# Weights of the values projection loaded into idle stage tiles, their splits between halves of a block, and gates stepped at each row tile

## The chip, the cores and the metric

The kernel runs on one core of a Trainium2 chip. The time is the device time of one execution in microseconds (us); lower is better. A run of the kernel gives one time, and the median over several runs is shown. Engines are named as in the profile: PE is TensorE (PEld its weight loads), DVE is VectorE, ACT is ScalarE, POOL is GpSimd. SP (SyncE) issues most of the DMAs; the rest are issued from ACT's and POOL's queues.

## The reference, cut to what matters

One encoder layer on x of 2048 rows by 1024 columns, in float32. The change lies in the first sub-layer's input projection and beside it:

```
hn = rms_norm(x, norm_mix_pre)
proj = hn @ w_in                          # 2048 x 3600
cv = short_conv3(proj[..., :2560], conv_w, conv_b)
q, k = silu(cv[..., 0:512]), silu(cv[..., 512:1024]) * 128 ** -0.5   # 4 heads
v, o_gate = proj[..., 2560:3072], sigmoid(proj[..., 3072:3584])
gates = proj[..., 3584:3600] + b_gates    # input and forget gates, two directions, 4 heads
h_m = (mlstm(q, k, v, gates[0], log_sigmoid(gates[1])) + mlstm backwards) * o_gate
z = cv[..., 1024:1536]                    # Hyena group
z = cv[..., 1536:2048] * two_sided_fft_conv(z, filter 0)
z = cv[..., 2048:2560] * two_sided_fft_conv(z, filter 1)
x = x + rms_norm(concat(group_rms(h_m), group_rms(z)) @ w_out, norm_mix_post)
x = x + rms_norm(square(relu(rms_norm(x) @ w_mlp_in)) @ w_mlp_out)
```

In the mLSTM, running sums of log_sigmoid of the forget gate and running maxima over chunks of 128 rows (16 chunks) are turned into weights and a stabiliser before any head can be worked on.

## The kernel before, in words

Nearly every large product is made as three matmuls: each operand is split into a high part, rounded to fp32r (a cast on ACT, line 166), and the remainder (a subtract on DVE or POOL, line 169), and `mm3` (lines 154 to 161) issues low x high, high x low and high x high.

**The projection** (`project`, line 328) is a Python generator in two parts. The convolved part (`convolved`, line 559) makes the first 2560 columns, transposed, in 20 column tiles of 128 by 4 blocks of 512 rows; a block is three pieces of 9, 9 and 6 matmuls. The values part (`values_project`, line 660) makes the last 1040 columns, rows by columns, in four groups g of 260 columns in the order 3, 0, 1, 2 by 16 row tiles t of 128 rows; a block (one g, one t) is two halves of 12 matmuls of 260 columns, for k tiles 0 to 3 and 4 to 7. The running number of a block, 0 to 63, is i. Groups 0 and 1 hold the values, the end of 1, 2 and 3 the output gate (a sigmoid on ACT), and the last 16 columns of group 3 the gates.

**The weights** (`in_weights`, line 530) come in chunks of up to 520 columns in total. `fetch` loads a chunk from SP's queue into one of two raw tiles (tag wf). `chunk` multiplies it by the norm's weight on POOL (line 543), then casts it on ACT and subtracts on DVE into a pair of tiles (tags w0 and w1, four buffers each). A group of the values part has four chunks q of two k tiles each, a column tile of the convolved part two. A fetch into a raw tile must wait until the earlier chunk's split has read it, and a cast until the matmuls of the chunk four earlier have read its tile.

At a change of group in the values part (lines 734 to 743), chunks 0 and 1 of the next group are fetched after row tiles 9 and 11. After row tile 15 both are scaled and split, and behind each split a fetch of chunk 2 or 3 is issued; then chunks 2 and 3 are scaled and split. The first steps of the generator, up to line 684, do the same for group 3 while the convolved part ends: its last calls of `next(then)` (lines 569, 630, 640, 651 and 658) step the values generator.

**What sets the order.** From line 294 on the order of instructions on each engine is the order of the code. `drive` (line 217) weaves two generators: the Hyena pass with the loads of the first mLSTM head (`long_conv`, line 334) leads, and for each unit of time that it yields, the projection is stepped until it has yielded as much. So a yield such as the 4.0 in line 741 is a claim of time: the Hyena pass gets that much before the next block. The Hyena pass loads its operands from SP's queue three steps ahead (tag raw, six buffers), splits them on ACT, POOL and DVE, multiplies spectra in five DVE instructions of 64 or 128 rows by 512 (`product`, line 1111), and stores from ACT's queue. When it ends, `head_loads` puts 1 MB each of k, v and q in SP's queue, and `turned` makes the weighted keys from k and the gates.

**Stage tiles.** A convolved block's output stands in one of four tiles of tag yc (512 columns) until it is stored. In the values part the first of them is `gtile`: half of it takes the gate columns (`gin`, written by line 713), the other half two constants. The gates (`gates`, line 753) use three more, cut in tiles of 128 columns. A values block's output goes to a tile of tag vst (two buffers, two row tiles each) and is stored to DRAM from SP's queue.

**The gates** are a generator too, of some 20 steps: small matmuls with constants, a chain of some 12 DVE instructions with two scans, exponentials on ACT, and three round trips through DRAM (st_d, m_d, de_d; a store from ACT's queue, a load from SP's) that move values from partitions to rows. `values_project` steps them at every second row tile from i = 18 on (line 744). The results are `qt` and `decay` and a row of maxima in DRAM, `mrow`.

Of the kernel before, what the change touches and what calls it, by code (L numbers as in the profile page):

```python
# [8 lines left out]
F32 = mybir.dt.float32  # L9
# [138 lines left out]
class Builder:  # L148
# [381 lines left out]
    def in_weights(self, c0, n):  # L530

        wv = self.io["w_in"].rearrange("(k p) c -> p k c", p=128)
        nk = min(8, 520 // n)

        def fetch(q):
            raw = self.pw.tile([128, 520], F32, tag="wf", name="wf")[:, 0:nk * n].rearrange("p (k c) -> p k c", k=nk)
            self.load(raw, wv[:, nk * q:nk * q + nk, c0:c0 + n])
            return raw, self.nw[:, nk * q:nk * q + nk]

        def chunk(fetched):  # L540

            raw, nw = fetched
            self.pool.tensor_tensor(raw, raw, nw.unsqueeze(2).to_broadcast([128, nk, n]), ALU.mult)
            w = [self.pw.tile([128, 520], F32R, tag=f"w{e}", name=f"w{e}", bufs=4)[:, 0:nk * n]
                 .rearrange("p (k c) -> p k c", k=nk) for e in range(2)]
            self.split(w[0], w[1], raw)
            return w

        return fetch, chunk, 8 // nk

    @staticmethod
    def row_block(chunks, k):
# [6 lines left out]
    def convolved(self, cts, then):  # L559

        wk, hn, cw = self.pw, self.hn, self.cw
        pe, dve, act, pool = self.pe, self.dve, self.act, self.pool
        n = 4 * len(cts)
        fetched, weights, pts, ys, sts = {}, {}, {}, {}, {}

        def ahead(c, step):

            if c >= len(cts):
                next(then)
                return  # L570
            fetch, chunk, m = self.in_weights(128 * cts[c], 128)
# [14 lines left out]

        def centre(i):
            ct, b = of(i)
            yc = ys[i] = wk.tile([128, 512], F32, tag="yc", name="yc", bufs=4)
            act.activation(yc, pts[i], AF.Identity, scale=cw[:, ct, 1:2], bias=cw[:, ct, 3:4])  # L590

        def sides(i):
# [14 lines left out]
        def gated(i):  # L607
            if of(i)[0] < 8:
                act.activation(ys[i], ys[i], AF.Silu)
# [24 lines left out]
        for i in range(n + 3):  # L634
# [20 lines left out]
                stored(i - 3)  # L655
            if 2 <= i <= n + 1:
                gated(i - 2)
            yield 1.36 if i < n - 1 else 1.36 * live + next(then)

    def values_project(self):  # L660
# [1 line left out]
        wk, act, dve, N = self.pw, self.act, self.dve, 260  # L662
        raws, chunks, pts, sts = {}, {}, {}, {}

        def fetch(g, q):
            raws[g, q] = self.in_weights(2560 + N * g, N)[0](q)

        def chunk(g, q):
            chunks[g, q] = self.in_weights(2560 + N * g, N)[1](raws.pop((g, q)))

        bg = self.cp_bg
        self.load(bg, self.io["b_gates"].partition_broadcast(128))
# [1 line left out]
        fetch(3, 0)  # L674
        fetch(3, 1)
        yield 0.0
        for q in range(2):
            chunk(3, q)
            fetch(3, q + 2)
            yield 0.0  # L680
        chunk(3, 2)
        yield 0.0
        chunk(3, 3)
        yield 2.0

        self.gtile = wk.tile([128, 512], F32, tag="yc", name="gtile", bufs=4)
        self.gin = self.gtile[:, 0:256].rearrange("p (k c) -> p k c", k=2)
        gates = self.gates()

        def width(g):  # L690
# [2 lines left out]
        def block(g, t, ks):  # L693
            if ks[0] == 0:
                pts[g, t] = self.pp.tile([128, 512], F32, tag="pp", name="pt")[:, 0:N]
            for k in ks:
                self.mm3(pts[g, t], self.hn_tile(t, k), self.row_block([chunks[g, q] for q in range(4)], k), k == 0, k == 7)
# [23 lines left out]
                          sts.pop((g, t // 2))[:, :, 0:n])  # L721

        before, last, steps = None, None, [(g, t) for g in order for t in range(16)]
        for i, (g, t) in enumerate(steps):
            block(g, t, range(0, 4))
            if last:
                outputs(*last)
            yield 1.4
            block(g, t, range(4, 8))
            if before:  # L730
                stored(*before)
            before, last = last, (g, t)
            yield 1.4
            nxt = steps[min(i + 7, len(steps) - 1)][0]
            if nxt != g and t in (9, 11):
                fetch(nxt, t // 11)
            if nxt != g and t == 15:
                for q in range(2):
                    chunk(nxt, q)
                    fetch(nxt, q + 2)  # L740
                yield 4.0
                for q in range(2, 4):
                    chunk(nxt, q)
            if i >= 18 and i % 2 == 0:
                next(gates, None)
        outputs(*last)
        stored(*before)
# [5 lines left out]
    def gates(self):  # L753
# [18 lines left out]
        for kind, gs in enumerate((li, lf)):  # L772
            pt = bank()[:, 0, :]
# [1145 lines left out]
```

## Time and profile before

| what | value |
| --- | --- |
| time before, median of 3 runs (lowest to highest) | 2744.96 us (2743.41 to 2745.59) |
| the profiled execution's own time | 2740.85 us |
| its span in the profile | 2738.9 us, 35521 instructions |
| convolved part, last matmul | 718.5 us into the span |
| values part, first to last matmul | 730.5 to 1043.4 us |
| scaling of a chunk of weights on POOL (line 543), 56 of them | median 1042 ns |
| mean granted clock of PE over the span | 0.981 |

How to read it: the profile records one execution, instruction by instruction. Times in the views are from the start of the span. A row such as "PE pt L159 <- ACT w L166: 9.6, 3, 5.3" says that PE's instruction of line 159 that writes tile pt waited for ACT's instruction of line 166 that writes tile w, 9.6 us in all, three times, the longest 5.3. In rows in order of time the bracket holds how long the engine had been idle, and what ended that. The granted clock is the share of its full rate at which PE could run; 1.00 is full. Names of tiles: hn the normalised input, w the split weights, pt a block's bank of PSUM, py, p, pk, pu and pi those of the Hyena pass.

### The profile page before, as it was taken

The page shows a single profiled execution, that of the slowest core. Times are in us where ns is not written, and L with a number is a line of the kernel's source. Part 1 is how long each engine was busy: PE and PEld are TensorE (multiplying, and loading weights), DVE is VectorE, ACT ScalarE, POOL GpSimd, SP SyncE. Part 2 cuts the span into 40 slices and gives each one's busy share as a digit, 9 for nine tenths or more (in the row PEclk, how much of TensorE's full clock was granted, in tenths as well). Part 3 has the DMA queues.
Part 4 walks back from the last instruction along what each step waited for, and adds up shares of the span by engine and source line. Part 5 has one row for each costly group of instructions (what it writes and reads, how often), then busy time and mean ns, then how long its engine had stood idle before and what let it go on. Part 6 is the DMA issues. An engine that isn't in the chain of part 4 may idle for free.

```text
span 2738.9 us, 35521 instructions
## 1 busy us (share of the span) xinstructions
PE 2604.2 (95%) x12293; PEld 2125.6 (78%) x12293; DVE 1529.3 (56%) x2453; ACT 1239.9 (45%) x2301; POOL 1218.2 (44%) x973
## 2 busy tenths in 40 slices
PE   6999999999899998889997999989999999999998
PEld 5778888777788887767775788868888888888876
DVE  5676653777446654765555444464445443543578
ACT  6355544555434445653433544354454233232244
POOL 1221124554225542456675877777773340311232
PEclk9999999999999999999998999989999999999999
DMA  6233346565665648546756444453446553445546
GB/s 173 59 97 107 113 122 226 183 191 175 203 216 180 191 156 273 166 145 209 239 165 220 149 168 143 167 210 139 162 144 253 176 182 110 123 143 164 181 160 222
DMA packets 288355, 465.76 MB, mean 170 GB/s; under 512 B 37542, under 2 KB 149414, under 8 KB 287152
## 3 DMA queue, kind: packets, MB, share of 16 engines
q1 hardware_dynamic: 227600, 324.85, 37.9%
q10 hardware_dynamic: 53264, 117.53, 11.4%
q0 software_dynamic: 7312, 21.11, 3.0%
q8 instruction: 98, 1.61, 0.2%
q14 instruction: 81, 0.66, 0.1%
HBM read 289.27 MB, written 174.13 MB: 169 GB/s over the span
## 4 chain that ended last, share of the span: by engine, by line
PE 40%; DVE 5%; POOL 3%; ACT 2%; DMA 2%; issue 2%; ACTq 0%; DVEq 0%; POOLq 0%; SPq 0%
PE pm L160 13%; PE pm L161 13%; PE pm L159 13%; DVE cb L169 1%; DVE hm L169 1%; POOL xt L1222 1%; ACT xo L1360 1%; DMA m<-in_w_mlp_out_dram 0%; DVE hm L1844 0%; POOL cb L169 0%; DVE xo L1363 0%; DMA hm<-ht 0%; ACTq L234 0%; DVE gss L1264 0%; POOL ht L1395 0%
## 5 line engine op out<-in xcount | busy, mean ns | idle before, releaser
L166 ACT CAST cb<-m 128x1024 fp32r<-128x1024 f32 (+1 forms) x346 | 281.3, 847 | 443.7 <-PE pm L159 388.6
L169 DVE TENSOR_TENSOR cb<-m,cb 128x1024 fp32r<-128x1024 f32 (+1 forms) x222 | 239.5, 1116 | 301.1 <-ACT cb L166 300.8
L160 PE MATMUL pm<-hm,cb 128*128 128x512 f32 x896 | 355.2, 396 | 18.8 <-DVE hm L169 14.7
L159 PE MATMUL pm<-hm,cb 128*128 128x512 f32 x896 | 354.5, 396 | 9.2 <-POOL cb L169 4.1
L161 PE MATMUL pm<-hm,cb 128*128 128x512 f32 x896 | 353.8, 395 | 0.0
L160 PE MATMUL pm<-cb 128*128 128x512 f32 x880 | 344.0, 391 | 6.5 <-DVE cb L169 6.5
L159 PE MATMUL pm<-cb 128*128 128x512 f32 x880 | 342.6, 390 | 1.0 <-DVE cb L169 1.0
L161 PE MATMUL pm<-cb 128*128 128x512 f32 x880 | 343.1, 390 | 0.0
L169 POOL TENSOR_TENSOR cb<-m,cb 128x1024 fp32r<-128x1024 f32 x124 | 268.7, 2180 | 71.0 <-ACT cb L166 71.0
L1656 DVE TENSOR_TENSOR m<-pm,m 128x512 f32<-128x512 f32 x224 | 154.4, 690 | 258.0 <-PE pm L161 231.3
L159 PE MATMUL pt<-hn,w 128*128 128x512 f32 x640 | 269.4, 421 | 1.0 <-ACT hn L486 0.9
L160 PE MATMUL pt<-hn,w 128*128 128x512 f32 x640 | 253.9, 397 | 0.7 <-DVE hn L487 0.7
L161 PE MATMUL pt<-hn,w 128*128 128x512 f32 x640 | 252.8, 395 | 0.0
L169 POOL TENSOR_TENSOR raw<-raw,hi 128x512 fp32r<-128x512 f32 x160 | 205.6, 1298 | 104.4 <-ACT hi L166 79.3
L160 PEld LDWEIGHTS pm<-hm,cb 128*128 128x128 f32 x896 | 170.6, 190 | 60.0 <-DVE hm L169 18.0
L159 PEld LDWEIGHTS pm<-hm,cb 128*128 128x128 f32 x896 | 170.7, 191 | 49.8 <-POOL cb L169 6.1
L160 PEld LDWEIGHTS pm<-cb 128*128 128x128 f32 x880 | 165.5, 188 | 44.0 <-DVE cb L169 9.8
L161 PEld LDWEIGHTS pm<-hm,cb 128*128 128x128 f32 x896 | 170.7, 191 | 36.3
L159 PEld LDWEIGHTS pm<-cb 128*128 128x128 f32 x880 | 165.4, 188 | 35.9 <-ACT junk L1829 1.4
L161 PEld LDWEIGHTS pm<-cb 128*128 128x128 f32 x880 | 165.6, 188 | 34.3
L1660 ACT ACTIVATE m<-m 128x512 f32<-128x512 f32 x128 | 80.5, 630 | 221.4 <-DVE m L1656 214.9
L159 PE MATMUL pt<-w,hn 128*128 128x260 f32 x512 | 156.8, 306 | 9.6 <-ACT w L166 9.6
(322 smaller groups left out, 5572.5 us busy)
## 6 DMA issues: line engine op xcount, KB each, us to landing
ga<-m ACTq DMA_DIRECT2D x96, 512.0 KB
m<-ga SPq DMA_DIRECT2D x96, 512.0 KB
d<-st ACTq DMA_DIRECT2D x64, 512.0 KB
m<-in_w_mlp_in_dram SPq DMA_DIRECT2D x62, 512.0 KB
m<-in_w_mlp_out_dram SPq DMA_DIRECT2D x114, 256.0 KB
raw<-d SPq DMA_DIRECT2D x96, 256.0 KB
xt<-in_x_dram SPq DMA_DIRECT2D x32, 512.0 KB
dk<-kst SPq DMA_DIRECT2D x32, 512.0 KB
```

The lines of the kernel that those rows point to most:

```text
L159: pe.matmul(ps, w[1], x[0], start=first, stop=False)
L160: pe.matmul(ps, w[0], x[1], start=False, stop=False)
L161: pe.matmul(ps, w[0], x[0], start=False, stop=last)
L166: self.act.copy(hi, src)
L169: (eng_lo or self.dve).tensor_tensor(lo, src, hi.bitcast(F32), ALU.subtract)
L1222: eng.tensor_tensor(res[:, cs], tmp[e], res[:, cs], ALU.add)
L1360: act.activation(x1, xt, AF.Square, accum_out=ss1[:, h:h + 1])
L1656: dve.tensor_tensor(dst, a, b, ALU.add)
L1660: act.activation(g, g, AF.Relu)
```

## The change

Five edits, all in the projection and the gates:

- `in_weights` gives the scaling as a function of its own, and `fetch` can be told another tile than the raw ones. Stage tiles become 520 columns wide so that a chunk fits.
- At a change of group, chunks 2 and 3 of the next group are fetched at row tiles 9 and 11 as well, into two stage tiles. For group 1 only chunk 2 is; its chunk 3 takes a raw tile after chunk 0's split. Chunks are scaled at row tiles 12, 13 and 14, and after 15.
- The casts and subtracts of chunks 0 and 1 stand between the two halves of the block of row tile 15, those of 2 and 3 behind it. The yield of 4.0 there is kept for group 1 alone, and one of 1.0 is added for all.
- The generator of the values is stepped once more, at the end of the convolved block n - 4, and its first steps are cut differently: a fetch of chunk 2 goes with chunk 1's split, one of chunk 3 a step later.
- The gates are stepped at every row tile from i = 18, and finished at i = 40 if they are not. `gtile` goes: the gate columns go to `qt`, whose final contents are written later, and `mt` becomes the tile of `cm`.

```diff
@@ in_weights
-        def fetch(q):
-            raw = self.pw.tile([128, 520], F32, tag="wf", name="wf")[:, 0:nk * n].rearrange("p (k c) -> p k c", k=nk)
+        def fetch(q, place=("wf", 2)):
+            raw = self.pw.tile([128, 520], F32, tag=place[0], name="wf", bufs=place[1])[:, 0:nk * n].rearrange("p (k c) -> p k c", k=nk)
...
-        def chunk(fetched):
+        def scale(fetched):
             raw, nw = fetched
             self.pool.tensor_tensor(raw, raw, nw.unsqueeze(2).to_broadcast([128, nk, n]), ALU.mult)
+
+        def chunk(fetched, scaled=False):
+            raw = fetched[0]
+            if not scaled:
+                scale(fetched)
             w = [self.pw.tile([128, 520], F32R, tag=f"w{e}", name=f"w{e}", bufs=4)[:, 0:nk * n]
...
@@ convolved
-            yc = ys[i] = wk.tile([128, 512], F32, tag="yc", name="yc", bufs=4)
+            yc = ys[i] = wk.tile([128, 520], F32, tag="yc", name="yc", bufs=4)[:, 0:512]
...
+            if i == n - 4:
+                next(then)
             yield 1.36 if i < n - 1 else 1.36 * live + next(then)
@@ values_project
         fetch(3, 0)
         fetch(3, 1)
         yield 0.0
-        for q in range(2):
-            chunk(3, q)
-            fetch(3, q + 2)
-            yield 0.0
+        chunk(3, 0)
+        yield 0.0
+        chunk(3, 1)
+        fetch(3, 2)
+        yield 0.0
+        fetch(3, 3)
+        yield 0.0
         chunk(3, 2)
         yield 0.0
         chunk(3, 3)
         yield 2.0
-        self.gtile = wk.tile([128, 512], F32, tag="yc", name="gtile", bufs=4)
-        self.gin = self.gtile[:, 0:256].rearrange("p (k c) -> p k c", k=2)
+        self.gin = self.qt[:, 0:2, :]
...
+        yc = "yc", 4
         for i, (g, t) in enumerate(steps):
+            nxt = steps[min(i + 7, len(steps) - 1)][0]
+            new = nxt != g
             block(g, t, range(0, 4))
             if last:
                 outputs(*last)
             yield 1.4
+            if new and t == 15:
+                chunk(nxt, 0, True)
+                chunk(nxt, 1, True)
             block(g, t, range(4, 8))
             if before:
                 stored(*before)
             before, last = last, (g, t)
             yield 1.4
-            nxt = steps[min(i + 7, len(steps) - 1)][0]
-            if nxt != g and t in (9, 11):
-                fetch(nxt, t // 11)
-            if nxt != g and t == 15:
-                for q in range(2):
-                    chunk(nxt, q)
-                    fetch(nxt, q + 2)
-                yield 4.0
-                for q in range(2, 4):
-                    chunk(nxt, q)
-            if i >= 18 and i % 2 == 0:
+            if i == 40:
+                for _ in gates:
+                    pass
+            if new and t == 9:
+                fetch(nxt, 0)
+                fetch(nxt, 2, yc)
+            if new and t == 11:
+                fetch(nxt, 1)
+                if nxt != 1:
+                    fetch(nxt, 3, yc)
+            if new and t in (12, 13, 14):
+                scale(nxt, t - 12)
+            if new and t == 15:
+                if nxt == 1:
+                    fetch(nxt, 3)
+                else:
+                    scale(nxt, 3)
+                chunk(nxt, 2, True)
+                if nxt == 1:
+                    yield 4.0
+                chunk(nxt, 3, nxt != 1)
+                yield 1.0
+            if i >= 18:
                 next(gates, None)
@@ gates
-        free = [self.gtile[:, 256:384], self.gtile[:, 384:512]]
+        free = []
         for _ in range(3):
-            t = self.pw.tile([128, 512], F32, tag="yc", name="gt", bufs=4)
+            t = self.pw.tile([128, 520], F32, tag="yc", name="gt", bufs=4)
...
-        rev, permt, li, lf, e, u, l1, rc, ones, bc, r, cm, mt = free[0:13]
+        rev, permt, li, lf, e, u, l1, rc, ones, bc, r, cm = free
+        mt = cm
...
-        dve.tensor_copy(mt, pt)
-        self.store(self.mrow, mt)
+        dve.tensor_copy(rc, pt)
+        self.store(self.mrow, rc)
```

More of the change, by code (lines that the diff above doesn't have):

```diff
@@ L547, in chunk @@
             return w
-        return fetch, chunk, 8 // nk
+        return fetch, chunk, 8 // nk, scale
     @staticmethod
@@ L570, in ahead @@
                 return
-            fetch, chunk, m = self.in_weights(128 * cts[c], 128)
+            fetch, chunk, m, _ = self.in_weights(128 * cts[c], 128)
             if step == 0:
@@ L663, in values_project, with fetch, scale, chunk @@
         raws, chunks, pts, sts = {}, {}, {}, {}
[L665 to L669, printed above, removed]
+        def fetch(g, q, *place):
+            raws[g, q] = self.in_weights(2560 + N * g, N)[0](q, *place)
+        def scale(g, q):
+            self.in_weights(2560 + N * g, N)[3](raws[g, q])
+        def chunk(g, q, scaled=False):
+            chunks[g, q] = self.in_weights(2560 + N * g, N)[1](raws.pop((g, q)), scaled)
         bg = self.cp_bg
```

## The prediction

> **What bounds the kernel now.** I read three views in turn: the page (which engine is full), the table by stretches over the projection's last 400 us (where that engine is not full), and the waits and rows in order of time there (what it waits for).
>
> ```profile
> PE 2604.2 (95%) x12293; PEld 2125.6 (78%) x12293; DVE 1529.3 (56%) x2453; ACT 1239.9 (45%) x2301; POOL 1218.2 (44%) x973
> ```
>
> The page says that PE is busy 95% of the span. In such a kernel a change that moves no matmul can win only stretches in which PE stands still, or runs at a lower clock. So the next view is where those are. Columns: window, length, busy time of PE, PEld, DVE, ACT, POOL, granted clock, DMA share, GB/s.
>
> ```profile
> 680.00:700.00 20.00, 20.00 (x85) 15.53 (x84) 8.67 (x16) 6.87 (x11) 0.00 (x0) 1.00 0.66 211
> 700.00:720.00 20.00, 18.35 (x76) 13.73 (x74) 12.08 (x19) 8.19 (x16) 8.18 (x7) 1.00 0.25 72
> 720.00:740.00 20.00, 13.89 (x70) 11.43 (x71) 10.52 (x19) 10.95 (x19) 5.88 (x5) 0.83 0.79 284
> 800.00:820.00 20.00, 14.52 (x107) 13.50 (x105) 5.35 (x13) 5.17 (x10) 2.06 (x2) 0.93 0.44 152
> 840.00:860.00 20.00, 20.00 (x139) 17.62 (x137) 14.61 (x29) 9.66 (x17) 7.75 (x8) 1.00 0.59 182
> 880.00:900.00 20.00, 17.59 (x104) 14.18 (x103) 14.60 (x25) 10.70 (x21) 13.38 (x14) 1.00 0.72 219
> 960.00:980.00 20.00, 14.67 (x82) 11.66 (x82) 13.31 (x21) 8.01 (x18) 12.11 (x12) 0.94 0.50 162
> 1040.00:1060.00 20.00, 13.55 (x87) 12.42 (x86) 4.75 (x10) 10.26 (x33) 2.52 (x5) 0.82 0.95 293
> ```
>
> PE is full in the rows from 680 and from 840. The holes are the hand-over from the convolved part to the values part (7.8 us idle in 700 to 740), the three changes of group in the values part (5.5, 2.4 and 5.3 us) and the start of the mLSTM (6.5 us). The waits say whose they are: total, times, longest.
>
> ```profile
> PE pt L159 <- ACT w L166: 9.6, 3, 5.3
> PE py L159 <- ACT hi L166: 5.5, 3, 3.5
> PE pk L159 <- ACT z L1104: 2.2, 1, 2.2
> PE pt L160 <- DVE w L169: 1.5, 3, 0.7
> SPq L231 <- DVE w L169: 24.4, 4, 11.1
> ```
>
> The first and fourth are PE waiting for the split of the next group's weights, the last is SP's queue standing still because a fetch of weights waits until a split has emptied its buffer. The rows in order of time put them in place (start, length, what, idle before it):
>
> ```profile
> 717.99 0.38 SPq L231 DMA_DIRECT2D wf<-in_w_in_dram  x1
> 723.10 0.50 PE L159 MATMUL py<-hi,c 128*128 128x512 f32 x1 [3.45 <-ACT hi L166]
> 812.68 1.03 SPq L231 DMA_DIRECT2D wf<-in_w_in_dram  x2
> 817.43 2.06 POOL L543 TENSOR_TENSOR wf<-wf,nw 128x520 f32<-128x520 f32 x2 [20.99 <-DMA wf<-in_w_in_dram]
> 819.19 0.58 PE L159 MATMUL pt<-w,hn 128*128 128x260 f32 x1 [5.25 <-ACT w L166]
> 896.27 0.39 PE L159 MATMUL pt<-w,hn 128*128 128x260 f32 x1 [1.73 <-ACT w L166]
> 971.47 0.47 PE L159 MATMUL pk<-hi,c 128*128 128x512 f32 x1 [2.22 <-ACT z L1104]
> 977.34 0.44 PE L159 MATMUL pt<-w,hn 128*128 128x260 f32 x1 [2.64 <-ACT w L166]
> ```
>
> At the first change of group the second half of the weights is fetched at 812.68, once the first half is split; it is scaled at 817.43, and PE starts at 819.19. That whole chain is what the change loads ahead. The hand-over's hole has another owner: a fetch of weights leaves SP at 717.99, behind a split, and the Hyena loads queued behind it come late to the cast on which PE waits until 723.10.
>
> Idle time is followed by matmuls at a lower clock (the third column from the end):
>
> ```profile
> 704.00:708.00 4.00, 2.98 (x13) 1.88 (x11) 1.94 (x4) 2.47 (x5) 2.12 (x2) 1.00 0.13 16
> 708.00:712.00 4.00, 3.73 (x15) 2.76 (x16) 1.83 (x3) 1.37 (x3) 0.00 (x0) 1.00 0.88 310
> 724.00:728.00 4.00, 1.62 (x3) 0.58 (x3) 1.90 (x3) 2.56 (x5) 2.42 (x3) 0.62 0.87 321
> 728.00:732.00 4.00, 3.77 (x13) 3.28 (x14) 3.81 (x9) 2.64 (x6) 1.17 (x1) 0.53 0.45 151
> 819.20:822.00 2.80, 2.47 (x9) 2.17 (x10) 1.70 (x4) 2.48 (x7) 1.60 (x3) 0.50 0.24 84
> 822.00:826.00 4.00, 4.00 (x28) 4.00 (x28) 0.43 (x1) 0.89 (x2) 4.00 (x5) 0.76 0.59 171
> 976.00:980.00 4.00, 2.19 (x9) 1.94 (x10) 1.90 (x3) 1.86 (x5) 1.64 (x2) 0.69 0.61 211
> 980.00:984.00 4.00, 4.00 (x26) 3.75 (x26) 2.08 (x4) 2.64 (x7) 3.00 (x3) 0.88 0.32 94
> ```
>
> Busy time times what the clock lacks is the loss. It is 1.62 x 0.38 + 3.77 x 0.47 = 2.4 us at the hand-over, 2.47 x 0.5 + 4.00 x 0.24 = 2.2 us after the first change of group, and 2.19 x 0.31 + 4.00 x 0.12 = 1.2 us after the third.
>
> **The change part by part.** The costs of one chunk, and PE's pace (shortest, median, longest; below, two neighbouring matmuls of the values part):
>
> ```profile
> L543 POOL TENSOR_TENSOR wf<-wf,nw x56: 1033/1042/1498, 18.5 to 976.6; 128x512 f32<-128x512 f32 x40, 128x520 f32<-128x520 f32 x16
> L166 ACT CAST w<-wf x56: 607/621/640, 19.5 to 977.7; 128x512 fp32r<-128x512 f32 x40, 128x520 fp32r<-128x520 f32 x16
> L169 DVE TENSOR_TENSOR w<-wf,w x56: 675/692/1442, 22.7 to 978.3; 128x512 fp32r<-128x512 f32 x40, 128x520 fp32r<-128x520 f32 x16
> 1043.24 0.29 PE L160 MATMUL pt<-w,hn 128*128 128x260 f32 x1
> 1043.36 0.28 PE L161 MATMUL pt<-w,hn 128*128 128x260 f32 x1
> ```
>
> A matmul starts every 0.12 us, so half a block (12 of them) is 1.44 us. No arithmetic of the reference goes or comes: the same scalings, splits, fetches and matmuls are issued elsewhere.
>
> *Hand-over.* The values generator is stepped once earlier, so chunk 0 of group 3 is scaled and split one block earlier, while POOL is idle (0.00 in the row from 680), and the fetch of chunk 2 stands a step later than chunk 0's split, chunk 3's a step later than chunk 1's. Then neither waits in SP's queue, and the Hyena loads behind them leave when their buffers come free. The 3.45 us and most of the two stalls behind it go. What is late next: chunks 2 and 3 are still scaled and split among the Hyena operands, and the cast of chunk 2 waits on ACT for POOL. One chunk's passage (1.04 + 0.62 + 0.69 = 2.35 us) lies ahead of the next Hyena operand, so I keep that as a stall; I also keep the 1.3 us of small stalls between 704 and 712 (1.02 and 0.27 in the rows above), which are of the Hyena pass itself. Saved: 7.8 - 1.3 - 2.35 = 4.1 us idle and the 2.4 us of clock: 6.5 us. Bounds: 2 (SP's stall shrinks but operands stay late) to 10 (all).
>
> *First change of group* (3 to 0). All four chunks are in SBUF by row tile 11, two of them in stage tiles that nothing else uses then. The scalings lie on POOL, which has 2.1 us of work in 20 here. After the first half of block 15 the casts of chunks 0 and 1 start; DVE ends at about 0.62 + 2 x 0.69 = 2.0 us, while PE has 1.44 us of the second half and 0.72 us of chunk 0's k tiles. Chunks 2 and 3 follow in 2 x 0.69 more, by 3.5 us, and PE needs them at 2.9 and 3.6. The Hyena pass issues nothing here, since its next loads wait for stores. Saved: 5.5 idle and 2.2 of clock, 7.7 us; bounds 5 to 8.
>
> *Second change* (0 to 1). The gate tiles hold three of the four stage tiles, so only chunk 2 goes ahead; chunk 3 is fetched when chunk 0 is split, and its scaling queues on POOL behind two Hyena prepares, its subtract on DVE behind two Hyena products. That is the order of before, and I take the 2.4 us to stay; bounds -2 (one more product in front) to +2.4.
>
> *Third change* (1 to 2). Loaded ahead like the first; the gates are through by row tile 37, so the stage tiles are free at 41. In before the chunks' casts stand on ACT ahead of the copy of a spectrum, and wait there for POOL: that is the 2.22 us at 971.47, then 2.64 us for the second pair. In the new order POOL has scaled three of the four, and between block 15's first half and the first use of chunk 2 PE has two more Hyena products and three halves, about 6 us, against 3.5 us of splits. Saved: 5.3 idle and 1.2 of clock, 6.5 us; bounds 3 to 6.5.
>
> *Gates at each row tile.* 20 steps from row tile 18 now end at 37 and no longer at 56. The instructions are the same; store and load of each DRAM round trip stand two row tiles apart, and load and use one; 16 row tiles lie between the restarts at 819.19 and 896.27, so these are 9.6 and 4.8 us. I cost it at nothing: DVE has 14.61 us of work in 20 in the row from 840, and covers it; without that cover it is the slower rival below. Renaming two gate tiles (the running maximum in place, gin in the tile of the results) moves no instruction.
>
> *Order against the Hyena pass.* The generator now claims 1 + 5 + 1 units at the changes of group, where it claimed 4 + 4 + 4. So 5 units less of its time are empty, and values work runs ahead: counting the yields of both versions, 6 halves of blocks follow the loads of the first mLSTM head in before, 3 in after. The rows there:
>
> ```profile
> 1031.13 1.02 PE L1144 MATMUL pi<-z,ci 128*128 128x512 f32 x2
> 1032.80 0.33 ACTq L234 DMA_DIRECT2D d<-st  x1
> 1035.62 0.33 SPq L231 DMA_DIRECT2D k<-qk  x1
> 1047.71 2.45 PE L957 MATMUL pS<-q,k 128*128 128x128 f32 x16 [3.63 <-DMA q<-qk]
> 1048.66 0.67 ACT L708 ACTIVATE vst<-pt 128x260 f32<-128x260 f32 x2 [10.35 <-DMA vo<-vst]
> ```
>
> The last Hyena matmuls, their store, the loads of k, v and q and the first scores are one chain, 16.6 us from 1031.13 to 1047.71, and PE already waits 3.63 us for its end. Three halves now stand in front of that chain, not beside it: 3 x 1.44 = 4.3 us are given back, as more idle time before the scores. Against it, ACT's 10.35 us wait ends: the store that it waited for now goes ahead of the 3 MB of loads, so the head's casts and the last store come earlier. PE still waits for q, so I take only 1 us for it; bounds -1 to 5.
>
> **Sum.** 6.5 + 7.7 + 0 + 6.5 - 4.3 + 1 = 17.4 us. The profiled execution took 2740.85 us, 4.1 less than the median shown, and holes of this kind are in each execution; so the 17.4 goes off the median, 2744.96: about 2727.6 us.
>
> The Trainium skill, TensorE: Matmul & The Clock Gate (Part 1, What's actually happening), lets the clock fall only after an idle window of about 3.4 us. By that rule the third change, whose stalls are 2.22 and 2.64 us with matmuls between them, would have no clock to win back, and the sum would be 16.2 us, 2728.8. The rows from 976 (0.69 and 0.88) speak against a strict reading.
>
> **The rivals.** *Splits held on the in-order engines.* The early casts stand on ACT ahead of Hyena casts and wait there for PE to leave the weight tile. If that, or a product in front of them on DVE, costs at each change what the second costs now (2.4 us), the first and third win 5.3 and 4.1; with 4 at the hand-over, and nothing at the mLSTM's start, 4 + 5.3 + 4.1 - 4.3 = 9.1 us: 2735.9. For it: the row at 971.47 is such a case. Against it: at the first change the Hyena pass is silent, and at the third PE has 6 us of cover. The Trainium skill, TensorE: Matmul & The Clock Gate (Part 1, Architectural detail), states that ACT and DVE are strict FIFO, which is this rival's rule; the trace agrees at 971.47.
>
> *Given back.* Only the first change works (7.7), the hand-over stays bound by the Hyena operands, the third keeps its stalls because POOL comes late, and the end takes its 4.3: 3.4 us, 2741.6, no change by the measure below.
>
> *Slower: the gates on DVE.* Place: row tiles 18 to 37, 20 x 4.8 = 96 us, in which DVE has (20 - 14.61) / 20 of the time to spare, 26 us. A gate step has work of its own and makes DVE wait in order for a matmul, an exponential or a landing. Above 1.3 us in each of the 20 steps the spare time is gone, and Hyena products come late to PE. It eats the whole gain from 17.4 + 26 = 43 us on, 2.2 us a step; at 2.6 us a step (52 us) the loss is 26 us, net 8.6: 2753.6. Against it: before runs such a step at every second row tile there already, and PE is full in the row from 840.
>
> **How the numbers follow.** The forecast 0.64, splits held 0.22, given back 0.09, slower 0.05. About 0.2% (5.5 us) is what a measurement of this kernel can tell from no change. The forecast's own bounds, when not all of them fall together, are 2718 to 2734; the range goes up to take in the held splits: 2717 to 2740. Faster by over 0.2% (under 2739.5): 0.64 + 0.22 and a little of the third, 0.87; within 0.2%: 0.08; slower: 0.05.
>
> **What would show it.** In the profile after: SP's waits for DVE w gone; no PE wait for ACT w over 1 us at the first and third change, one of 1 to 3 us at the second; clock 1.00 after both; the first scores still waiting for q, for some 7 us or more; ACT's wait for the values store gone. The forecast is wrong if new PE waits for DVE or ACT appear between 820 and 930, where the gates now run, or if the mLSTM's start moves by less than 10 us.

## The result, and the profile after

| | before | after |
| --- | --- | --- |
| median (lowest to highest, runs) | 2745.47 us (2743.41 to 2747.03, 6) | 2719.70 us (2713.61 to 2724.55, 6) |
| profiled execution, its span | 2740.85 us, 2738.9 us | 2723.08 us, 2721.3 us |

The ratio is 0.9905, 95% interval 0.9894 to 0.9917: 25.8 us faster, where 17.4 were forecast. The two profiled executions differ by only 17.8 us, because the one of before lies 4.6 below its median and the one of after 3.4 above. That must be kept in mind when one trace is read against the other.

The engines in the page of after have the same work and a shorter span:

```profile
PE 2602.7 (96%) x12293; PEld 2125.3 (78%) x12293; DVE 1527.1 (56%) x2453; ACT 1237.2 (45%) x2300; POOL 1220.3 (45%) x973
```

The table by stretches of after, with the columns of the prediction's:

```profile
700.00:720.00 20.00, 17.95 (x69) 13.60 (x68) 11.62 (x20) 10.34 (x19) 8.37 (x8) 0.91 0.49 157
720.00:740.00 20.00, 19.78 (x114) 16.46 (x113) 11.81 (x21) 13.62 (x21) 6.34 (x6) 1.00 0.76 254
800.00:820.00 20.00, 20.00 (x160) 19.60 (x159) 5.74 (x15) 7.81 (x16) 5.96 (x6) 1.00 0.49 156
840.00:860.00 20.00, 20.00 (x133) 17.38 (x132) 14.59 (x28) 8.77 (x17) 11.85 (x12) 1.00 0.82 245
860.00:880.00 20.00, 19.54 (x123) 16.42 (x122) 13.58 (x26) 11.03 (x25) 11.31 (x11) 1.00 0.85 185
880.00:900.00 20.00, 17.51 (x106) 14.99 (x106) 14.15 (x29) 8.49 (x17) 10.18 (x11) 0.91 0.52 168
960.00:980.00 20.00, 20.00 (x137) 17.79 (x137) 14.29 (x22) 9.42 (x22) 11.71 (x11) 1.00 0.64 196
```

PE is now full in the rows from 800 (14.52 busy before) and from 960 (14.67 before), both at a clock of 1.00: the first and the third change of group have no hole left. The hand-over has 2.05 + 0.22 = 2.3 us idle where it had 7.8. What remains is in the row from 880, at the second change. DVE, which the slower rival feared for, is as busy in 840 to 860 as it was (14.59 against 14.61), and PE is full in that row.

The waits of after's SP queue from 690 to 1045, and of PE from 690 to 1095 (those that bear on the change, and the longest):

```profile
SPq L231 <- DVE w L169: 6.1, 1, 6.1
```

```profile
PE ps L1008 <- ACT nm L1015: 4.0, 3, 2.5
PE pt L159 <- ACT w L166: 2.1, 1, 2.1
PE ptk L945 <- DVE kw L952: 2.1, 1, 2.1
PE ptk L945 <- DMA k<-qk: 1.5, 1, 1.5
PE py L159 <- ACT hi L166: 1.0, 1, 1.0
PE pt L160 <- DVE w L169: 0.3, 1, 0.3
```

PE's first row lies inside the mLSTM. SP stood 24.4 us in four waits for a split to empty a buffer; it now stands 6.1 in one, where the prediction had none left. PE's three waits for the cast of the next weights have become one, at the second change. ACT's 10.35 us wait for a values store is gone. And there is a line that the prediction did not have: at the mLSTM's start PE waits 1.5 us for k and no longer for q. The rows in order of time (start, length, what, idle before it), all of after but the last, which is of before:

```profile
708.96 0.50 PE L159 MATMUL py<-hi,c 128*128 128x512 f32 x1 [1.03 <-ACT hi L166]
885.14 0.39 PE L159 MATMUL pt<-w,hn 128*128 128x260 f32 x1 [2.15 <-ACT w L166]
1027.87 0.63 PE L945 MATMUL ptk<-eye,k 128*128 128x128 f32 x4 [1.46 <-DMA k<-qk]
1030.57 1.12 PE L945 MATMUL ptk<-eye,k 128*128 128x128 f32 x4 [2.06 <-DVE kw L952]
1036.52 1.06 PE L990 MATMUL pS<-q,k 128*128 128x128 f32 x8
1043.48 0.60 PE L912 MATMUL ptk<-eye,k 128*128 128x128 f32 x4
```

The keys of the first head are transposed on PE (ptk) and then scaled. After turns twelve of the sixteen ahead of the first scores (pS), which then wait for nothing. In before only the four of the row at 1043.48 went ahead, and the scores waited 3.63 us for q.

**Two points that divide the time.** The last Hyena product (pi) and the last product of the mLSTM (pa) are the same matmuls in both kernels. Their groups, before and then after; the two numbers behind the durations are the starts of the first and the last one:

```profile
L1144 PE MATMUL pi<-z,ci x128: 590/592/592, 495.7 to 1031.6; 128*128 128x512 f32 x128
L977 PE MATMUL pa<-v,pm x256: 272/275/422, 1068.9 to 1191.7; 128*128 128x129 f32 x128
```

```profile
L1177 PE MATMUL pi<-z,ci x128: 590/592/668, 497.2 to 1018.6; 128*128 128x512 f32 x128
L1010 PE MATMUL pa<-v,pm x256: 272/275/422, 1047.5 to 1173.8; 128*128 128x129 f32 x128
```

Hyena, first to last: 535.9 us before, 521.4 after. From there to the first pa: 37.3 before, 28.9 after; to the last pa: 160.1 before, 155.2 after. Everything behind it is alike: pa ends 17.9 us earlier, the span 17.6.

The second stretch in one row for each kernel, from the last pi to the end of the mLSTM, before and then after:

```profile
1031.60:1192.40 160.80, 134.28 (x921) 121.14 (x919) 97.26 (x263) 97.08 (x328) 65.34 (x75) 0.95 0.62 198
```

```profile
1018.60:1174.40 155.80, 132.63 (x884) 119.81 (x882) 96.34 (x263) 96.21 (x326) 65.20 (x75) 0.92 0.65 203
```

The counts show the halves of blocks: 921 matmuls against 884 are the three halves of 12 that now run earlier (one record is missing). So 4.3 us of work have left this stretch, as forecast. But PE's idle time in it did not rise by them: it is 26.5 us before and 23.2 after. The clock is lower in this one execution of after (0.92), which hides a part of the gain.

### The profile page after: what moved, and what is told of

Same layout as the page of the kernel before. It is cut to its first block, busy times and chain, and to the rows that moved or that the text cites. A ratio compares the mean times of both kernels' runs of the same rounds, so it can differ in the third digit from the quotient of the medians.

```text
span 2721.3 us, 35529 instructions
## 1 busy us (share of the span) xinstructions
PE 2602.7 (96%) x12293; PEld 2125.3 (78%) x12293; DVE 1527.1 (56%) x2453; ACT 1237.2 (45%) x2300; POOL 1220.3 (45%) x973
## 4 chain that ended last, share of the span: by engine, by line
PE 40%; DVE 5%; POOL 3%; DMA 3%; ACT 2%; issue 2%; ACTq 0%; DVEq 0%; POOLq 0%; SPq 0%
PE pm L160 13%; PE pm L161 13%; PE pm L159 13%; DVE cb L169 1%; POOL xt L1255 1%; DVE hm L169 1%; ACT xo L1393 1%; DMA m<-ga 1%; DVE hm L1877 0%; DMA m<-in_w_mlp_out_dram 0%; POOL cb L169 0%; DMA hm<-ht 0%; DVE xo L1396 0%; POOL ht L1428 0%; DVE hm L1807 0%
## 5 line engine op out<-in xcount | busy, mean ns | idle before, releaser
L169 DVE TENSOR_TENSOR cb<-m,cb 128x1024 fp32r<-128x1024 f32 (+1 forms) x222 | 232.5, 1084 | 306.0 <-ACT cb L166 296.3
L635 POOL DMA_DIRECT2D vp<-vst x96 | 61.3, 642 | 232.0 <-ACT vst L631 230.9
```

The source lines that it names most:

```text
L169: (eng_lo or self.dve).tensor_tensor(lo, src, hi.bitcast(F32), ALU.subtract)
L635: pool.dma_start(dst[:, 8 * b + e:8 * b + 8:2, cc:cc + 128], st[64 * e:64 * e + 64])
```

## The experiments

Theory A is the recorded sum: the holes give 20.7 us, three halves of blocks are given back at the mLSTM's start (4.3), and 1 is won there. Theory B: the start of the mLSTM itself became shorter, so the price of 4.3 is none; it first named ACT's wait for the values store as the cause. The kernel before was run again beside each group of experiments, with medians of 2748.76, 2751.69 and 2750.38 us on three chips; so ratios are compared, and 0.0010 is 2.7 us.

**The hand-over alone**, in the kernel before, and **the change without it**:

```diff
+            if i == n - 4:
+                next(then)
...
-        for q in range(2):
-            chunk(3, q)
-            fetch(3, q + 2)
-            yield 0.0
+        chunk(3, 0)
+        yield 0.0
+        chunk(3, 1)
+        fetch(3, 2)
+        yield 0.0
+        fetch(3, 3)
+        yield 0.0
```

> Before with the hand-over's part of the change alone (the generator of the values stepped once more, its first steps cut anew). Theory A (the change wins what PE stood still at the hand-over and at the changes of group, hole by hole, as the sum has it): 6.5 us of the sum, so 2739 against 2745.5, a ratio of 0.9976; SP's wait for a split gone, PE's 3.45 us stall before 723 gone. Theory B (a good part of the 25.8 us comes from the new order of values work against the Hyena pass and its effect on the mLSTM's start): hand-over worth 4 us or less, 2741.5 or more.

> After with the hand-over's part undone. Theory A (holes add up): the 3.45 us stall is back, and the time stands 6 to 9 us above after, as the hand-over alone won 9: a ratio to before of 0.9930 to 0.9940 where after has 0.9905. Rival (the parts overlap, since the same Hyena pass is hurried): 3 us or less above after, 0.9905 to 0.9915.

The first gave 2741.53 us, ratio 0.9967 (0.9954 to 0.9979): 9 us won. The second, after with these lines as before, gave 2728.15, 0.9910 (0.9897 to 0.9924), against 0.9905 for the change as a whole: 1.4 us lost, its error some 5. The errors of the two only meet at 5 to 6 us, near the 6.5 of the sum. The trace of the second shows the old stall again:

```profile
726.00 0.49 PE L159 MATMUL py<-hi,c 128*128 128x512 f32 x1 [3.94 <-ACT hi L166]
```

In the first that row is gone, and the first change's hole is still 5.79 us at 814.10. So the stall goes with this edit, which both steps the generator once more and moves the fetches; the two were not tried apart. Its price in the whole is known to a few us only.

**The gates at every row tile alone**, in the kernel before:

```diff
-            if i >= 18 and i % 2 == 0:
+            if i >= 18:
                 next(gates, None)
```

> Before with the gates stepped at each row tile from 18, nothing else. Theory A: the steps are covered, 0 +- 1.5 us (2744 to 2747). Theory C (gates done earlier are themselves worth something, or cost DVE time on PE's path): faster than 2743 or slower than 2748; slower would show as new PE waits for DVE between 820 and 930.

2746.42 us, 0.9993 (0.9984 to 1.0001). The holes at the changes of group were as in before (5.55 us at 822.69). Within this interval the edit neither costs nor wins anything by itself; it makes the stage tiles free for the loads of the third change.

**Group 2 loaded as before**, the other changes as in after (chunks 2 and 3 fetched behind row tile 15 into raw tiles, with the claim of 4.0 there). Chunks 0 and 1 stay scaled and split early, as in after:

```diff
-                fetch(nxt, 2, yc)
+                if nxt != 2:
+                    fetch(nxt, 2, yc)
...
+                if nxt == 2:
+                    fetch(nxt, 2)
+                    fetch(nxt, 3)
+                    yield 4.0
+                    chunk(nxt, 2)
+                    chunk(nxt, 3)
```

> After with the third change of group loaded as in before (chunks 2 and 3 fetched behind the splits of 0 and 1, 4 units claimed between). Theory A: its stalls (2.2 and 2.6 us) and the low clock behind them are back: 5 to 7 us above after, 0.9925 to 0.9930. Rival (that hole is filled by Hyena work once the others run ahead): within 2 us of after.

2732.06 us, 0.9926 (0.9913 to 0.9938): 5.8 us of the gain lost, with an error of some 5; the sum had 6.5. About half of the idle time is back (2.8 us in 960 to 980, where before had 5.3), at a lower clock (0.83), and so is the wait for q at the mLSTM's start:

```profile
960.00:980.00 20.00, 17.16 (x93) 14.43 (x92) 10.98 (x16) 8.04 (x20) 9.72 (x10) 0.83 0.54 170
965.14 0.39 PE L159 MATMUL pt<-w,hn 128*128 128x260 f32 x1 [2.18 <-ACT w L166]
1038.14 2.07 PE L998 MATMUL pS<-q,k 128*128 128x128 f32 x8 [5.11 <-DMA q<-qk]
```

The size agrees with the third change's term, but this run moves two things at once: with the larger claim, five halves follow the loads of the first head instead of three. Which of the two cost the 5.8 us it doesn't tell.

**The splits behind the block**: after, but with the casts of chunks 0 and 1 behind the second half of block 15, not between its halves.

```diff
-            if new and t == 15:
-                chunk(nxt, 0, True)
-                chunk(nxt, 1, True)
             block(g, t, range(4, 8))
...
             yield 1.4
+            if new and t == 15:
+                chunk(nxt, 0, True)
+                chunk(nxt, 1, True)
```

> After with the casts and subtracts of chunks 0 and 1 behind block 15 and not between its halves. Holes theory: chunk 0's cast and subtract (0.62 + 0.69 us) stand bare at the first change, chunk 1's partly: one PE wait for ACT w or DVE w of 0.5 to 1.5 us there, none at the third, where Hyena products stand between; 1 to 2 us slower than after. Rival of the prediction (splits set early hold the queues of ACT and DVE): faster than after by 2 us or more.

2722.06 us, 0.9901 (0.9885 to 0.9917); after itself, run a second time beside it on the same chip, had 2720.64 and 0.9897 (0.9881 to 0.9913). PE shows no wait for w at the first or third change, where 0.5 to 1.5 us were expected at the first, and 1.85 us at the second. So the place of the splits did nothing that can be seen: the early load and scaling are enough to close the holes.

> After once more, beside its variants on one chip: 0.9895 to 0.9915 to before. It measures the chip, no theory.

**The claims of time alone**, in both directions. First the kernel before with the claims of after (1 + 5 + 1 for 4 + 4 + 4), all loads as they were; then after with the claims of 4.

```diff
-                yield 4.0
+                yield 5.0 if nxt == 1 else 1.0
```

```diff
-                yield 1.0
+                if nxt != 1:
+                    yield 4.0
```

> Before with the claims of time at the changes of group as in the change (1, 5 and 1 units for 4, 4 and 4), nothing else. Theory A: holes stay, the one at the third change grows by 1 to 3 us since less Hyena work stands in it, and the end gives back about what the earlier store of values wins: 2745 to 2749. Theory B: 2740 or less, with the mLSTM's first product of states 5 us or more earlier than its holes explain.

> After, but with 4 units claimed at each change of group as in before, so that 6 halves of blocks follow the loads of the first mLSTM head again. Theory A as put on record (4.3 us given back at the end for 1 won): 3.3 us faster than after, 2716.4. Theory B: the earlier store is worth more than the three halves, so this is slower than after by 3 to 8 us, 2723 to 2728, with ACT's wait for the store of values (10.35 us in before) back.

Here theory A falls. The first keeps all three holes and should by A have won nothing, or lost; it took 2741.55 us, 0.9968 (0.9956 to 0.9981), 8.8 us less than before. The second should by A have won 3.3 us over after; it took 2726.35, 0.9913 (0.9897 to 0.9928), 2 us more, with an error of some 5, so that this run alone speaks only weakly against A. In the trace of the first kernel the holes stand, and its last pi is later than before's, but the mLSTM starts as in after:

```profile
821.05 0.59 PE L159 MATMUL pt<-w,hn 128*128 128x260 f32 x1 [5.76 <-ACT w L166]
979.31 0.58 PE L159 MATMUL pt<-w,hn 128*128 128x260 f32 x1 [3.10 <-ACT w L166]
1050.70 0.63 PE L912 MATMUL ptk<-eye,k 128*128 128x128 f32 x4 [1.46 <-DMA k<-qk]
```

In the second the waits of before are back, on ACT 10.6 us for a values store, and on PE:

```profile
1033.86 3.67 PE L991 MATMUL pS<-q,k 128*128 128x128 f32 x16 [3.79 <-DMA q<-qk]
```

**Is it ACT's wait for the store?** The kernel before, with the stores of the last three pairs of row tiles of values issued from ACT's queue, so that they don't stand behind the 3 MB of loads in SP's:

```diff
-                self.load(self.vo[...], sts.pop((g, t // 2))[:, :, 0:n])
+                put = self.store if (g, t) in ((2, 11), (2, 13), (2, 15)) else self.load
+                put(self.vo[...], sts.pop((g, t // 2))[:, :, 0:n])
```

> Before with the last three stores of values (row tiles 10 to 15 of group 2) issued from ACT's queue, so that they don't stand behind the 3 MB of loads of k, v and q; nothing else. Theory B (the wait of ACT for that store holds the start of the mLSTM): ACT's 10.35 us wait goes, the first product of states comes 6 to 9 us earlier after the last Hyena matmul (36.8 us in before), and the time falls by 6 to 9 us, 0.9967 to 0.9978. Theory A as recorded: PE waits for q all the same, 0 to 1 us.

2750.86 us, 0.9994 (0.9986 to 1.0003): nothing. The 10.35 us wait was gone from the trace, and the first pa came 33.0 us after the last pi, 4.3 sooner than in before; but the last pa came 161.4 us after it, as late as in before. So B's first cause does not explain the gain. One place where the 4.3 us go back shows in PE's rows: it waits 4.44 us for a scaled key (kw) at 1107.01, where before waited 1.18 (the second row). That this wait is the reason is not shown.

```profile
1107.01 0.80 PE L934 MATMUL pv<-v,kw 128*128 128x129 f32 x2 [4.44 <-ACT kw L918]
1103.83 0.49 PE L933 MATMUL pv<-v,kw 128*128 128x129 f32 x2 [1.18 <-ACT kw L917]
```

At the start, where the wait had been, another instruction stood in ACT's way, the exponential of the maxima, ahead of the scalings of keys (line 918). ACT's rows:

```profile
1053.26 1.14 ACT L918 ACTIVATE kw<-ptk,qt 128x128 f32<-128x128 f32 x4 [1.53 <-PE ptk L913]
1056.67 1.28 ACT L961 ACT_TABLE_LOAD   x1 [2.27 <-DMA mb<-mrow]
1057.97 0.40 ACT L961 ACTIVATE mb<-mb,qt 128x128 f32<-128x128 f32 x1
1058.28 1.12 ACT L918 ACTIVATE kw<-ptk,qt 128x128 f32<-128x128 f32 x4
```

**The second change loaded ahead too**, with its chunk 3 in a stage tile as well; four of the gates' tiles go to `qt`, so that the gates need two stage tiles and not three:

```diff
-                if nxt != 1:
-                    fetch(nxt, 3, yc)
+                fetch(nxt, 3, yc)
...
-                if nxt == 1:
-                    fetch(nxt, 3)
-                else:
-                    scale(nxt, 3)
+                scale(nxt, 3)
                 chunk(nxt, 2, True)
-                if nxt == 1:
-                    yield 4.0
-                chunk(nxt, 3, nxt != 1)
-                yield 1.0
+                chunk(nxt, 3, True)
+                yield 5.0 if nxt == 1 else 1.0
...
-        for _ in range(3):
+        for _ in range(2):
...
-        rev, permt, li, lf, e, u, l1, rc, ones, bc, r, cm = free
+        rev, permt, li, lf, rc, ones, bc, cm = free
+        e, u, l1, r = (self.qt[:, i, :] for i in range(4))
```

> After with group 1's chunk 3 loaded ahead as well; four gate tiles move into the tile of the results so that two stage tiles are free; the claims of 1, 5 and 1 units stay. Theory A: the 2.15 and 0.34 us at the second change go, and the low clock behind them: 3 to 4 us faster than after, 0.9890 to 0.9895, with no PE wait for a split left in the values part. Rival (DVE's product is what PE waits for there, whatever is loaded): as after.

> The version with all four chunks ahead at each change once more, on the same chip as after. Holes theory: 3 to 6 us faster than after (2.5 us idle and the low clock behind it), 0.9875 to 0.9895. Rival (the first comparison was the chip): within 2 us of after.

2719.13 us, 0.9880 (0.9867 to 0.9894), and again, beside after, 2715.99 us (2715.49 to 2718.28), 0.9878 (0.9862 to 0.9894), where after's runs lay from 2718.30 to 2726.48. It is the best of all versions together with the next one, about 5 us under after. PE's wait of 2.15 us has become 0.20, and in the row from 880 PE is busy 19.67 us at a clock of 1.00 (the second of these runs):

```profile
886.16 0.39 PE L159 MATMUL pt<-w,hn 128*128 128x260 f32 x1 [0.20 <-DVE gt L856]
```

```profile
880.00:900.00 20.00, 19.67 (x129) 17.13 (x130) 15.99 (x32) 9.69 (x21) 10.82 (x13) 1.00 0.53 176
```

**No halves behind the loads at all**: the kernel just shown with a claim of 1.0 at every change.

```diff
-                yield 5.0 if nxt == 1 else 1.0
+                yield 1.0
```

> The same with 1 unit claimed at the second change too (1, 1 and 1), so that no half of a block is left behind the loads of the first mLSTM head. The recorded price of values work set ahead of the Hyena pass's end (1.44 us for each half): the last Hyena matmul 4 us later against the same point, PE's wait for k 4 us longer (1.4 to 5.5 us), 3 to 4.5 us slower than the version with 1, 5 and 1. Rival (that the new order at the mLSTM's start wins by itself, the more the earlier values work ends): as fast or faster.

2715.81 us, 0.9876 (0.9858 to 0.9893): the same as with three halves. The trace shows the recorded price, in part made good by the clock. Its row of the second stretch (849 matmuls, three halves fewer again), and PE's wait:

```profile
1020.30:1169.90 149.60, 120.65 (x849) 107.52 (x847) 97.46 (x263) 95.68 (x325) 64.80 (x70) 0.97 0.66 208
1030.18 1.09 PE L940 MATMUL ptk<-eye,k 128*128 128x128 f32 x4 [6.39 <-issue]
```

Idle time is 28.9 us here, against 25.4 and 22.1 in the two profiles with three halves, and PE waits 6.39 us before the first key, where it waited about 1.4: the last three halves are given back as the prediction had it. The clock in the stretch is 0.97 where it was 0.95, and the work is 4.3 us less; the last pa stands at 1169.3 against 1171.5 and 1166.9.

## Why the prediction was right, and which step of it was wrong

The sign, the place and the range were right; the time was 7.9 us lower than forecast, near the range's fast end. Of the other signs, the clock of 1.00 at the first and third change and the end of ACT's wait came, and between 820 and 930, where the gates now run, PE has no wait longer than about 0.5 us but the one of the second change. Taking the terms in turn, by the profiles of before and after (idle from the windows, clock as in the prediction). The clock that after still lost stands in these rows of it:

```profile
708.00:712.00 4.00, 2.02 (x6) 1.12 (x7) 2.72 (x4) 3.23 (x6) 1.64 (x2) 0.95 0.41 131
712.00:716.00 4.00, 4.00 (x13) 3.14 (x12) 2.65 (x6) 1.14 (x2) 0.91 (x1) 0.62 0.94 279
884.00:888.00 4.00, 2.51 (x9) 2.13 (x10) 1.64 (x4) 1.59 (x3) 0.43 (x1) 0.71 0.34 136
888.00:892.00 4.00, 4.00 (x22) 3.30 (x21) 2.85 (x6) 2.23 (x5) 0.46 (x1) 0.86 0.51 166
```

That is 2.02 x 0.05 + 4.00 x 0.38 = 1.6 us at the hand-over and 2.51 x 0.29 + 4.00 x 0.14 = 1.3 us after the second change.

| term | forecast | measured: idle + clock |
| --- | --- | --- |
| hand-over | 6.5 | 5.5 + 0.8 = 6.3 |
| first change | 7.7 | 5.6 + 2.2 = 7.8 |
| second change | 0 (-2 to 2.4) | -0.5 - 1.3 = -1.8 |
| third change | 6.5 | 5.3 + 1.2 = 6.5 |
| start of the mLSTM | -4.3 + 1 = -3.3 | about +3, below |

The four holes give 18.8 us. The first Hyena stretch says the same: 14.5 us shorter although 4.3 us more of values work stand in it. Before's profile is one of its shorter executions; by the middles of three profiles below the holes give 21.8, so the four terms together are good to some 3 us.

*The hand-over.* Right in the total, in part by luck. The stall of one chunk that I kept at 2.35 us is not there; 1.03, 0.85 and 0.17 us around 709 are, so 1.4 us more of idle time went than forecast. But all 2.4 us of clock were to come back, and the rows after these stalls still lose 1.6. The two errors cancel.

*The first and third changes.* Right, as worked out, by the rows of after. No run leaves the first change alone as it was, so its 7.8 us are read from the trace and not from a time. The 1.44 us of cover between the halves of block 15 was not what did it, since the kernel with the splits behind the block had no wait there either.

*The second change.* The wait stayed, as forecast. The sum had no clock term here, and after has one: the wait for the cast is 2.15 us where it was 1.73, and the rows from 884 stand at 0.71 and 0.86, where before's row from 880 had 1.00.

*The gates.* Nothing beyond the error, as costed, by the run that had them alone. The slower rival had no part.

*The start of the mLSTM* is the failed step: "Three halves now stand in front of that chain, not beside it: 3 x 1.44 = 4.3 us are given back, as more idle time before the scores." The halves went where the count had them. But what PE did while q landed changed: twelve keys were turned ahead of the scores instead of four, and the first scores no longer wait for q. "The first scores still waiting for q, for some 7 us or more" is thus the sign that failed. Single profiles differ by several us here, so all are used, by the number of halves that follow the loads of the first head (as the prediction counts them; PE's rows have two more behind the last pi in every kernel: 96, 84, 60 and 24 matmuls):

| halves | kernels | last pi to first pa, us | last pi to last pa, us | PE idle to the end of the mLSTM, us |
| --- | --- | --- | --- | --- |
| 6 | before, hand-over alone, gates alone, store moved, after with claims of 4 | 37.3, 37.6, 36.9, 33.0, 37.0 | 160.1, 161.2, 160.3, 161.4, 162.7 | 26.5, 28.8, 29.0, 27.7, 30.6; mean 28.5 |
| 5 | group 2 as before | 37.2 | 160.7 | 24.7 |
| 3 | after (twice), claims alone, no hand-over, late splits, second change ahead (twice) | 28.9, 29.1, 28.1, 28.0, 29.1, 28.2, 28.2 | 155.2, 152.5, 150.1, 152.8, 153.1, 155.3, 151.0 | 23.2, 21.5, 19.9, 22.2, 23.2, 25.4, 22.1; mean 22.5 |
| 0 | claims of 1 | 28.9 | 149.0 | 28.9 |

By both distances, every kernel with three halves is below every one with five or six. From six to three the whole stretch loses 8.3 us on average and the part up to the first pa 7.9, so the change lies in the start; from the first to the last pa it takes 124.8 us with six halves and 124.4 with three. Of the 8.3, 4.3 are work that stands earlier; so some 4 are won. PE's idle time was to rise by 4.3. It falls by 6 in the whole stretch, and in the start alone from a mean of 8.6 to 5.9. From three to none the recorded price does come: the start takes as long as with three halves, with 4.3 us less work in it, and its idle time is 10.4 us. The term that was -3.3 is about +3 to +4.

**The sum again, by middles of three profiles.** Two experiments ran as long as before, and their Hyena stretch was longer than in before's own profile: 538.9 and 540.0 us against 535.9, middle 538.9; second stretch 160.1, 160.3 and 161.4, middle 160.3. After, its repetition and the late splits: 521.4, 521.4 and 521.1, and 155.2, 152.5 and 153.1, middles 521.4 and 153.1. That makes 17.5 and 7.2 us, together 24.7, with 25.8 by the medians. Against the recorded 17.4 it is +1.1 for the holes (17.5 + 4.3 = 21.8 against 20.7) and +6.2 for the mLSTM's start (7.2 - 4.3 = 2.9 against -3.3).

**What stays open.** That the mLSTM's start gets shorter with the smaller claims is shown, by the claims alone in before (28.1 us to the first pa for 37.3). Why it does is not: the new order on PE and ACT (twelve keys turned ahead of the scores, not four), or the values' end being nearer to the last pi. The traces speak for the order. In five profiles the first scores come behind four keys, and the first pa stands 36.9 to 37.6 us after the last pi; with the store moved they come behind eight, and it is 33.0; in the other eight profiles they come behind twelve, and it is 28.0 to 29.1. Going from six halves to five, or from three to none, without a change of this order, moves it by less than 1 us. But no run changes the order alone. ACT's wait for the store alone does not explain the gain. The hand-over's own share, 1.4 us or 9, was not settled either. The claims and the hand-over each won about 9 us alone in before, though the three changes of group kept their holes, and less at the end of the whole change; so the parts tried singly do not add up to 25.8.

**The clock after short stalls.** In the row from 884 of after the clock is 0.71, behind stalls of 2.15 and 0.34 us. The Trainium skill, TensorE: Matmul & The Clock Gate (Part 1, What's actually happening), asks for an idle window of about 3.4 us before the clock falls. The prediction doubted a strict reading, and this row speaks against it too. The same section says that the window runs free, so that the same kernel loses differently from run to run; the last section has such a difference, but no trace here shows that the window is its cause.

## What to carry to other kernels

Where PE is nearly full, list its holes by their owner and ask for each what would have to be in SBUF earlier: buffers that are idle at just that time take the load, and a fetch that waits for a buffer is moved behind the step that empties it, so that nothing queues behind it. When work moves across a seam between stages, don't price the seam by the chain that ended last before: look at what else the engine could do during that wait, and try the move by itself, since here it was worth as much as one of the holes. One profile each is not enough for the rest of the sum; profiles of kernels that run equally long tell how far one execution strays.

## What was not expected of the hardware

The clock in the mLSTM differs from execution to execution of one kernel. In steps of 5 us from the last pi to the end of the mLSTM, busy time by what the clock lacks sums to 9.9 us in after's profile and 7.9 in its repetition, to 7.1 in before and 2.3 in the kernel with claims of 1. The stalls there are many and short. The six runs of after spread over 11 us, from 2713.61 at a mean clock of 0.986 to 2724.55 at 0.981. Single rows in that stretch fall to 0.83 without a hole of their own, as the second of these of after; the ten us ahead of it had 2.47 us idle at 1.00:

```profile
1148.00:1158.00 10.00, 7.53 (x52) 6.37 (x51) 4.96 (x13) 4.98 (x19) 7.04 (x6) 1.00 0.28 74
1158.00:1168.00 10.00, 10.00 (x54) 8.56 (x54) 5.75 (x17) 5.35 (x17) 5.33 (x4) 0.83 0.20 60
```

Removing a long wait need not win time. Moving the store took 10.35 us of waiting off ACT and the kernel ran no faster: the exponential in ACT's order then waited 2.27 us for a load ahead of the scalings of keys, and the 4.3 us by which the first pa came sooner were gone at the last. The Trainium skill, TensorE: Matmul & The Clock Gate (Part 1, Architectural detail), calls ACT strictly first in, first out. The rows at 1056.67 and 1058.28 agree.
